# Splitting weight blocks on VectorE alone in the mixers and at the stage ends of a two-block network

## The chip, the core and the metric

The kernel runs on one core of a Trainium2 chip. Five engines work side by side, each on its own queue in order: TensorE (PE; its weight loads are listed as PEld), VectorE (DVE), ScalarE (ACT), GpSimd (POOL) and SyncE (SP, which here only issues loads). Data lie in SBUF, matmul results in PSUM. The metric is the device time of one execution in microseconds, median of several runs.

## The reference

A sequence of 256 rows of width 1024, all in float32, goes through two blocks. The first block has two layers; each is a SwiGLU feed-forward (FFN), a mixer, and a second FFN, each followed by a residual and a layer norm:

```
x = layer_norm(ALPHA * x + 0.5 * swiglu(x, w1, w2))
proj = x @ w_in                       # b_gate, c_gate, v, x_r, y_r, g_logits
y_a = (b_gate * conv3(c_gate * v)) @ w_out_conv
xc  = conv4(x_r) + rc_b;  gates = sigmoid(xc @ rg_w + rg_b)     # per head
y_b = (rg_lru(xc, gates) * gelu(y_r)) @ w_out_rnn
mix = (sigmoid(g_a) * y_a + sigmoid(g_b) * y_b) @ w_o
x = layer_norm(ALPHA * x + mix)
x = layer_norm(ALPHA * x + 0.5 * swiglu(x, w1', w2'))
```

The second block is one layer: modulation, RMS norm, a recurrence and an attention with selected keys, a projection with a residual, and a mixture of 16 experts behind a router in two levels.

## The kernel before

**Weights.** All weights are packed on the host into blocks of 128x1024 floats in the order of their use, two to a load of 1 MB. `Weights.load` (line 161) issues the loads on SP's queue into five raw buffers. A weight is used as a sum of two parts: `Weights.pump` (line 184) takes the next block `h` of the order, has ScalarE cast it to the matmul's type (line 197, the high part) and has VectorE or GpSimd subtract that from the raw block (line 202, the low part). This pair is called a split here. Six split buffers exist (`NSPLIT`); when TensorE is done with a block, `done` (line 272) releases its buffer and pumps the next, so that a split is made some five blocks ahead of its use. A raw buffer is given back when both of its blocks are split. Who subtracts is chosen by three lines of `pump`:

```
pool = self.gp and h % self.gp == 0
if 0 < self.lo <= h < self.lo + len(POOL):
    pool = POOL[h - self.lo] == "1"
```

`gp` is 0 at first: VectorE takes all. `mixer` sets it to `M_GP` = 2 (line 630), so that every second block goes to GpSimd. `tail`, the end of a stage, sets it to 1 (line 467, all to GpSimd) after the first half of the rows, and back to 0 (line 479) where it has begun the next stage. In the last `tail`, in front of the router, it stays 1 until line 1666. `lo` and the 38 digits of `POOL` (line 39) rule the first part of the second block instead.

**Matmuls.** An activation is held as high and low part too, transposed (`xT`: 2 parts x 8 column blocks x 256 rows). `ws` (line 320) multiplies a weight block by it in 24 matmuls of 256 columns: lines 323 to 325 use high x high, high x low, and low x high. `ts` (line 372) and `tz` (line 337) do it the other way round, with 512 columns.

**Mixer** (line 605 on). Two groups of four channel blocks. For two blocks at a time: y_r and x_r are projected; VectorE makes the convolution of four taps (lines 657 and 659), split for the gates by functions put into `soon`, which `done` runs one by one. Then c_gate and v; ScalarE copies one (line 728), VectorE multiplies (line 731), which frees the PSUM tile, and convolves (lines 733, 735). Behind the second of each pair the gate matmuls follow (`gates`, lines 674 to 676), which need PSUM tiles freed by line 731. The recurrence `lru` (lines 684 to 714, with the product by the gelu at line 711) is a generator, advanced by `done` in small steps. The second part of the mixer projects the merge logits, multiplies by the two output matrices (`merge`), and sums into the accumulators with w_o.

**End of a stage** (`tail`, line 435). The last five weight blocks are swept first for rows 0 to 127, then for rows 128 to 255. Between the two, `vec_fn(0)` puts the layer norm of the first half (`ln_vec`, lines 410 to 427) into VectorE's queue: lines 417 and 418 on each half of the columns, a square root on ScalarE, then lines 426 and 427 on each half. The second sweep then pumps new splits as it frees buffers. After it, TensorE transposes the first half (`to_xT`, line 393), ScalarE casts it (line 396) and VectorE makes the low part (line 388). That last step stands in the queue behind the first instructions of the second half's layer norm. `begin` starts the next stage's first four blocks for the first half (line 340), and the second half is transposed. Six stages end this way: FFN, mixer, FFN, twice. At the last of them an RMS norm with its weights follows the layer norm (`rms_in`, lines 505 to 509), and the splits stand in VectorE's or GpSimd's queue ahead of its multiplications (`rest`).

**Router** (`route`, line 1436). In front of the experts, `W.pump(NPRE)` (3 splits) stands ahead of `best_group` (lines 1415 to 1419 and 1426), whose result TensorE ranks (line 1428), and `W.pump(NPRE2)` (2 splits) at the end.

Of the kernel before, what the change touches and what calls it, by code (L numbers as in the profile page):

```python
# [57 lines left out]
ADA = 16  # L58
GATES = (1, 1)
NLAST = 2  # L60
M_WORK, M_GP = 1.2, 2
L_EXP, L_SQ, L_ROOT, L_MUL, L_SCAN = 99, 0.6, 1.0, 2, 0.5
NSPARE = 2
NPRE0, NPRE, NPRE2 = 0, 3, 2
# [166 lines left out]
def kernel(ctx, tc, x, blocks, vecs, lnrows, consts, rows, bias_w, wr, out):  # L231
# [7 lines left out]
    W = Weights(tc, blocks, order, raw_pool, split_pool)  # L239
# [32 lines left out]
    def done(n=1, pump=None, work=None):  # L272
        W.release(n)
        W.pump(n if pump is None else pump)
        if soon:
            soon.popleft()()
        step(M_WORK if work is None else work)
# [35 lines left out]
    def preload(func):  # L313
        nc.scalar.activation(tiny, eps[:, 0:1], func)
# [30 lines left out]
    def begin(keys, xT, mid=None):  # L345
        ps = [mm_tile(), mm_tile()]
        halves = []
        for q in range(4):
            halves.append(W.take(*keys[q]))
            tz(ps[0], 0, halves[q], q, xT)  # L350
            if mid and q == 1:
                mid()
                for k in range(2):
                    tz(ps[1], 1, halves[k], k, xT)
            elif mid and q > 1:
                tz(ps[1], 1, halves[q], q, xT)
        begun.append((ps, halves, xT, mid))
# [77 lines left out]
    def tail(keys, acts, acc, vec_fn, tr_fn, xn=None, plan=None):  # L435
        halves = [W.take(*k) for k in keys]
        last = len(halves) - 1

        def sweep(T, i, n):
            a = acts[i][:, :, T * 128:T * 128 + 128]  # L440
            for hx, hw in ((0, 0), (0, 1), (1, 0)):
                nc.tensor.matmul(acc[T][n], a[:, hx], halves[i][:, hw, n * 512:n * 512 + 512], start=False,
                                 stop=(i == last and hx == 1))

        def spent(T, i):
            if T:
                done(1, pump=int(len(W.split) < (4 if plan else NPRE0)), work=0)

        def half_pass(T, mid=None, rest=None):
            for i in range(last - NLAST + 1):  # L450
                for n in range(2):
                    sweep(T, i, n)
                spent(T, i)
            if rest:
                rest()
            for n in range(2):
                for i in range(last - NLAST + 1, last + 1):
                    sweep(T, i, n)
                    if n:
                        spent(T, i)  # L460
                if mid and n == 0:
                    mid()

        preload(AF.Sqrt)
        half_pass(0)
        rest = vec_fn(0, None)
        W.gp = 1
        if plan:
            half_pass(1, None, rest)
            after = tr_fn(0, mm_tile)  # L470
        else:
            half_pass(1, lambda: tr_fn(0, mm_tile))
            after = None
        rest = vec_fn(1, after)
        if rest:
            rest()
        if plan:
            begin(plan, xn)
            W.gp = 0
            tr_fn(1, acc_tile)()  # L480
        else:
            tr_fn(1, mm_tile)
# [33 lines left out]
    def ffn(l, j, xT, last):  # L516
# [82 lines left out]
        else:  # L599
            vf, tf = (lambda T, mid: ln_vec(T, acc, g, mid)), (lambda T, new: to_xT(xn, xres[:, T], T, new))  # L600
        plan = [("zt", Z_AQ, q) if last else ("em", l, q) if j == 0 else ("e1", l + 1, 0, q) for q in range(4)]
        tail([("w2", l, j, k) for k in ks], [hs[k] for k in ks], acc, vf, tf, xn, plan)
        return xn

    def mixer(l, xT):
# [164 lines left out]
        for i in range(8):  # L770
# [14 lines left out]
            if i >= 2 and i - 2 < 8 - NSTAG:  # L785
# [5 lines left out]
        xn = new_xT()  # L791
        ks = range(8 - NSTAG, 8)
        tail([("wo", l, k) for k in ks], [ms[k] for k in ks], acc, lambda T, mid: ln_vec(T, acc, g, mid),
             lambda T, new: to_xT(xn, xres[:, T], T, new), xn, [("e1", l, 1, q) for q in range(4)])
        return xn
# [683 lines left out]

    ksl = range(nk, 8)  # L1480
    tail([("wout", k) for k in ksl], [mixT[:, :, k] for k in ksl], acc, mix_vec, route)
    turn_[1] = False

# [186 lines left out]
    with tc.If(flag > 0):  # L1670
# [4 lines left out]
        W = W2  # L1675
# [132 lines left out]
```

## Time and profile before

| | |
|---|---|
| median of 3 runs | 1840.64 us (1839.89 to 1840.68) |
| the profiled execution, its own time | 1835.68 us |
| its span, first to last instruction | 1833.9 us |
| TensorE (PE) busy | 1738.9 us, 95% |
| VectorE (DVE) busy | 1304.2 us, 71% |
| ScalarE (ACT) busy | 975.0 us, 53% |
| GpSimd (POOL) busy | 376.9 us, 21% |
| splits on VectorE / GpSimd | 489 + 54 / 122 |
| mean granted TensorE clock | 0.982 |

The profile's times are us from the first instruction. A row of the timeline has the start, the length, the engine, the line of the kernel, the operation, what it writes and reads, the shapes, and in square brackets the engine's idle time before it with what ended it. Busy time of an engine that isn't the bottleneck costs nothing as long as no one waits for it.

### The profile page before, as it was taken

The numbers are of one execution on the slowest core, as the hardware profiler recorded it, in microseconds if no ns is written. First come the engines' busy times: TensorE is split into PE (matmuls) and PEld (weight loads), VectorE is DVE, ScalarE is ACT, GpSimd is POOL, SyncE is SP. The second block draws the span as 40 slices with busy tenths as digits, with TensorE's granted clock in tenths as the row PEclk, the third lists the DMA queues.
The fourth block names the chain that finished last, engine by engine and source line by source line (L and its number), as shares of the span: only waits on it lengthen the run. The fifth ranks groups of instructions, "written<-read, shape, count | busy, mean of one in ns | idle before, by whom it ended". The sixth has DMA issues, their size and how long they took to land. (4 is left out here: it accounts for less than half of the span.)

```text
span 1833.9 us, 27864 instructions
## 1 busy us (share of the span) xinstructions
PE 1738.9 (95%) x11369; PEld 1578.1 (86%) x11369; DVE 1304.2 (71%) x1631; ACT 975.0 (53%) x1340; POOL 376.9 (21%) x195
## 2 busy tenths in 40 slices
PE   8789999999999999999999999999799888999998
PEld 7779899999799989998999997999698666878776
DVE  6276778865856685667788557555778767998997
ACT  5154365644544444444646535444374557777775
POOL 0000144353300020001443543000256541000000
PEclk9989999999999999999999999999899999999999
DMA  7677654555556665675545554655342347989883
GB/s 296 168 266 252 228 173 152 204 190 193 205 183 256 243 236 194 248 257 207 184 161 184 207 185 171 223 184 186 118 172 92 144 169 256 357 323 337 332 318 141
DMA packets 57256, 394.26 MB, mean 215 GB/s; under 512 B 6912, under 2 KB 7216, under 8 KB 10912
## 3 DMA queue, kind: packets, MB, share of 16 engines
q1 hardware_dynamic: 52416, 375.94, 56.1%
q0 software_dynamic: 4128, 15.72, 3.0%
q8 instruction: 91, 1.49, 0.3%
q10 hardware_dynamic: 576, 0.74, 0.1%
q14 instruction: 45, 0.37, 0.1%
HBM read 389.20 MB, written 3.17 MB: 214 GB/s over the span
## 5 line engine op out<-in xcount | busy, mean ns | idle before, releaser
L202 DVE TENSOR_TENSOR split<-raw,split 128x1024 fp32r<-128x1024 f32 x489 | 645.2, 1332 | 298.9 <-ACT split L197 293.8
L197 ACT CAST split<-raw 128x1024 fp32r<-128x1024 f32 x611 | 628.2, 1048 | 248.1 <-PE mm L325 65.1
L202 POOL TENSOR_TENSOR split<-raw,split 128x1024 fp32r<-128x1024 f32 x122 | 317.6, 2613 | 992.3 <-ACT split L197 981.5
L323 PE MATMUL mmo<-xT,split 128*128 128x256 f32 x1248 | 354.1, 284 | 0.0
L324 PE MATMUL mmo<-xT,split 128*128 128x256 f32 x1248 | 353.6, 283 | 0.0
L325 PE MATMUL mmo<-xT,split 128*128 128x256 f32 x1248 | 353.4, 283 | 0.0
L325 PE MATMUL mm<-xT,split 128*128 128x256 f32 x968 | 274.1, 283 | 2.4 <-POOL split L202 2.4
L323 PE MATMUL mm<-xT,split 128*128 128x256 f32 x968 | 274.0, 283 | 0.0
L324 PE MATMUL mm<-xT,split 128*128 128x256 f32 x968 | 273.9, 283 | 0.0
L324 PEld LDWEIGHTS mmo<-xT,split 128*128 128x128 f32 x1248 | 239.6, 192 | 1.7
L323 PEld LDWEIGHTS mmo<-xT,split 128*128 128x128 f32 x1248 | 239.6, 192 | 1.7
L325 PEld LDWEIGHTS mmo<-xT,split 128*128 128x128 f32 x1248 | 239.5, 192 | 0.0
L376 PE MATMUL acc<-split,ht 128*128 128x512 f32 x816 | 199.9, 394 | 16.0 <-ACT split L197 15.8
L376 PEld LDWEIGHTS acc<-split,ht 128*128 128x128 f32 x816 | 149.8, 190 | 46.1 <-ACT split L197 16.0
L1536 PE MATMUL hp<-split,xg 128*128 128x512 f32 x768 | 187.7, 398 | 0.8 <-DVE split L202 0.8
L325 PEld LDWEIGHTS mm<-xT,split 128*128 128x128 f32 x968 | 185.4, 192 | 2.8 <-POOL split L202 2.8
L323 PEld LDWEIGHTS mm<-xT,split 128*128 128x128 f32 x968 | 185.4, 192 | 1.3
L324 PEld LDWEIGHTS mm<-xT,split 128*128 128x128 f32 x968 | 185.4, 192 | 1.3
L1536 PEld LDWEIGHTS hp<-split,xg 128*128 128x128 f32 x768 | 142.9, 188 | 34.8 <-DVE split L202 1.1
L1594 PE MATMUL y<-split,ht 128*128 128x512 f32 x360 | 87.2, 397 | 0.0
L1594 PEld LDWEIGHTS y<-split,ht 128*128 128x128 f32 x360 | 67.1, 188 | 15.8
L553 DVE SCALAR_TENSOR_TENSOR junk<-raw,cb 128x1024 f32<-128x1024 f32 x48 | 58.5, 1219 | 23.2 <-ACT cb L551 23.2
(454 smaller groups left out, 2276.6 us busy)
## 6 DMA issues: line engine op xcount, KB each, us to landing
raw<-in_w_dram SPq DMA_DIRECT2D x328, 1024.0 KB, 4.9
spare<-in_w_dram SPq DMA_DIRECT2D x27, 1024.0 KB, 4.9
lng<-in_ln_dram POOLq DMA_DIRECT2D x6, 1024.0 KB, 4.9
raw<-in_w_dram SPq DMA_DIRECT2D x4, 512.0 KB, 7.7
scr<-ext_s POOLq DMA_DIRECT2D x1, 2048.0 KB, 47.7
cb<-in_row_dram POOLq DMA_DIRECT2D x3, 512.0 KB, 5.6
norm<-mrow POOLq DMA_DIRECT2D x2, 512.0 KB, 4.6
braw<-scr POOLq DMA_DIRECT2D x2, 512.0 KB, 4.8
```

What stands on the lines that cost most here:

```text
L197: self.nc.scalar.copy(t[:, 0], r)
L202: eng.tensor_sub(t[:, 1], r, t[:, 0].bitcast(F32))
L323: nc.tensor.matmul(ps, w[:, 0, k], xT[:, 0, k], start=(k == 0), stop=False)
L324: nc.tensor.matmul(ps, w[:, 0, k], xT[:, 1, k], start=False, stop=False)
L325: nc.tensor.matmul(ps, w[:, 1, k], xT[:, 0, k], start=False, stop=(k == 7))
L376: nc.tensor.matmul(acc[T][n], a[:, hx], half[:, hw, n * 512:n * 512 + 512], start=(first and hx == 0 and hw == 0), stop=(last and hx == 1))
L553: nc.vector.scalar_tensor_tensor(junk, w, 1.0, cb, op0=ALU.mult, op1=ALU.mult, accum_out=modc[:, c:c + 1])
L1536: nc.tensor.matmul(ps, xgs[g][:, hx, k], wv[:, hw, kk], start=(k == 0 and hx == 0 and hw == 0), stop=(k == 7 and hx == 1))
L1594: nc.tensor.matmul(ys[g][n][:, 0:w], ht[:, hx, q], half[:, hw, o:o + w], start=(j == 0 and q == 0 and hx == 0 and hw == 0), stop=(j == 3 a ...
```

## The change

Two lines. `M_GP` becomes 0, so that the mixers give no split to GpSimd, and `tail` no longer sets `gp` to 1. With that, `gp` is 0 everywhere; the string `POOL` still rules its 38 blocks of the second block.

```diff
@@ -58,7 +58,7 @@
 ADA = 16
 GATES = (1, 1)
 NLAST = 2
-M_WORK, M_GP = 1.2, 2
+M_WORK, M_GP = 1.2, 0
 L_EXP, L_SQ, L_ROOT, L_MUL, L_SCAN = 99, 0.6, 1.0, 2, 0.5
 NSPARE = 2
 NPRE0, NPRE, NPRE2 = 0, 3, 2
@@ -464,7 +464,6 @@
         preload(AF.Sqrt)
         half_pass(0)
         rest = vec_fn(0, None)
-        W.gp = 1
         if plan:
             half_pass(1, None, rest)
             after = tr_fn(0, mm_tile)
```

## Rows read from the trace of the kernel before

**Rows 1.** Busy time by engine in two stretches; order PE, PEld, DVE, ACT, POOL, clock, DMA share, GB/s
```profile
240.00:460.00 220.00, 214.30 (x1740) 211.67 (x1739) 157.19 (x183) 121.03 (x178) 96.39 (x39) 1.00 0.52 186
...
971.50:975.00 3.50, 3.50 (x19) 3.50 (x18) 2.92 (x3) 1.53 (x4) 1.80 (x1) 0.51 0.82 300
```

**Rows 2.** Waits of TensorE over the program: us in total, times, longest
```profile
PE mm L393 <- DVE xres L427: 8.5, 4, 2.2
PE mm L393 <- DVE xn L509: 7.3, 1, 7.3
PE rank L1428 <- DVE goh L1419: 6.4, 1, 6.4
...
PE mm L674 <- DVE pc L731: 5.9, 2, 3.0
...
PE mm L325 <- POOL split L202: 4.5, 4, 1.3
```

**Rows 3.** Timeline of the first mixer, VectorE at 262 and 316 to 329 us, GpSimd
```profile
262.60 0.35 DVE L733 TENSOR_SCALAR cv<-pc,vec 128x256 f32<-128x256 f32 x1
...
316.34 2.60 DVE L202 TENSOR_TENSOR split<-raw,split 128x1024 fp32r<-128x1024 f32 x1 [1.05 <-ACT split L197]
...
319.08 2.28 DVE L657 TENSOR_SCALAR xc<-xp,vec 128x256 f32<-128x256 f32 x1
...
326.55 2.39 POOL L202 TENSOR_TENSOR split<-raw,split 128x1024 fp32r<-128x1024 f32 x1 [5.34 <-ACT split L197]
...
326.99 2.09 DVE L733 TENSOR_SCALAR cv<-pc,vec 128x256 f32<-128x256 f32 x1
```

**Rows 4.** Groups of VectorE, 240 to 460 us: count, busy us, mean ns, idle before
```profile
L202 DVE TENSOR_TENSOR split<-raw,split 128x1024 fp32r<-128x1024 f32 x37 | 66.9, 1809 | 46.6 <-ACT split L197 43.6 <-PE mm L325 2.8
L733 DVE TENSOR_SCALAR cv<-pc,vec 128x256 f32<-128x256 f32 x8 | 16.3, 2043 | 0.3
```

**Rows 5.** Groups of VectorE in the experts' stage, 1523 to 1834 us
```profile
L202 DVE TENSOR_TENSOR split<-raw,split 128x1024 fp32r<-128x1024 f32 x133 | 160.4, 1223 | 14.5 <-ACT split L197 12.8
```

**Rows 6.** Busy time of the splits (line 202) in two stretches: DVE, POOL, clock, DMA
```profile
214.00:482.00 268.00, 74.06 (x40) 122.68 (x47) 1.00 0.49 175
661.00:669.50 8.50, 0.00 (x0) 8.40 (x3) 0.90 0.37 125
```

**Rows 7.** Timeline of VectorE, 1127 to 1131 us: four splits in a row
```profile
1126.80 4.63 DVE L202 TENSOR_TENSOR split<-raw,split 128x1024 fp32r<-128x1024 f32 x4 [0.51 <-ACT split L197]
```

**Rows 8.** Timeline of a stage end, 660 to 668 us, VectorE and TensorE
```profile
660.04 0.75 DVE L426 SCALAR_TENSOR_TENSOR lns<-lns,lnmv,lng 128x512 f32<-128x512 f32 x1
...
661.50 2.90 DVE L426 SCALAR_TENSOR_TENSOR lns<-lns,lnmv,lng 128x512 f32<-128x512 f32 x1
...
664.43 2.73 DVE L427 SCALAR_TENSOR_TENSOR xres<-lns,lnmv,lng 128x512 f32<-128x512 f32 x1
...
667.21 0.66 PE L393 MATMUL mmo<-ident,xres 128*128 128x128 f32 x4 [2.08 <-DVE xres L427]
```

**Rows 9.** Timeline of GpSimd, 462 to 486 us, the end of the first mixer
```profile
468.75 10.82 POOL L202 TENSOR_TENSOR split<-raw,split 128x1024 fp32r<-128x1024 f32 x4 [8.15 <-ACT split L197]
```

**Rows 10.** Timeline of VectorE, 1296 to 1332 us, the last stage end of the first block
```profile
1310.56 3.43 DVE L505 TENSOR_TENSOR xn<-xres,norm 128x512 f32<-128x512 f32 x2
...
1323.63 1.29 DVE L505 TENSOR_TENSOR xn<-xres,norm 128x512 f32<-128x512 f32 x2
```

**Rows 11.** Timeline of VectorE, 1495 to 1532 us, the router
```profile
1509.11 1.28 DVE L1416 TENSOR_TENSOR rt<-rlg,rt 128x8 f32<-128x8 f32 x1
1510.42 2.26 DVE L1417 TENSOR_TENSOR rt<-rt,w 128x8 f32<-128x8 f32 x1
...
1512.92 2.06 DVE L1419 TENSOR_TENSOR goh<-w,rt 128x8 f32<-128x8 f32 x1
...
1529.39 0.17 DVE L1417 TENSOR_TENSOR rt<-rt,w 128x8 f32<-128x8 f32 x1
```

## The prediction

> **What bounds the kernel now.** I began with the page's busy times (the table ahead): TensorE is far above the others, so time can only be won where it stands still. Next I cut out the middle of the first mixer: in 220 us TensorE is busy 214.3, VectorE 157.2, GpSimd 96.4 [rows 1]. No helper is full there, and only 5.7 us of standing still can be won in that window. Third, the waits of TensorE over the whole program [rows 2]. Five of them lie where the edited lines act: transposes that wait for the normalised rows of a stage (8.5 us in 4 waits), the same at the last stage of the first block (7.3 us once), the router's ranking (6.4 us once), the gate matmuls of the mixers that wait for VectorE's convolution (5.9 us in 2), and matmuls that wait for a split made on GpSimd (4.5 us in 4). That last one is the only wait that names GpSimd; the others name VectorE.
>
> So the question is why VectorE is late there. Rows of one form, with and without GpSimd beside them, answer it. A 128x256 tensor_scalar at line 733 took 0.35 us at 262.60 us and 2.09 us at 326.99; in the second case a GpSimd split had started at 326.55 and lasted 2.39 us, to 328.94, and the VectorE row ends 0.14 us after that [rows 3]. The same form has a mean of 2043 ns over its eight rows in the window above, and VectorE's own split has 1809 ns [rows 4] against 1223 ns in the experts' stage, where GpSimd splits nothing [rows 5]. VectorE's long rows are thus mostly waits for a GpSimd split to end.
>
> **What the change moves.** Every first-block mixer has 47 GpSimd splits with the stage ends at its two sides [rows 6]; there are two mixers. Two further stage ends have 3 each [rows 6] (the second, at 1304 us, is alike), and the router has 5 (NPRE and NPRE2). That is 94 + 6 + 5 = 105 of the 122. The 17 that the POOL string places in the second block stay. ScalarE's casts, the loads and TensorE's work stay as they are; GpSimd's own DMAs find a free queue; a raw block is given back sooner, which costs nothing as the loads fill 0.52 of the DMA engines here [rows 1]. What is new is that each split stands in VectorE's queue, in program order: 1.22 us alone, 4.63 us for four in a row, so 1.14 us for each further one and 3.49 us for three [rows 5, 7].
>
> **Ends of the first block's FFN stages, three of this kind.** In `tail` VectorE normalises the upper half of the rows while TensorE runs the last sweeps. At 660.04 us an instruction of the chain takes 0.75 us; then GpSimd starts its three splits and the next two take 2.90 and 2.73 [rows 8]. These waits, 2.15 + 1.98 = 4.13 us, go. TensorE's wait of 2.08 us for that result at 667.21 [rows 8] goes too, but this isn't the gain: the three splits now stand on VectorE between the upper half's chain and the lower half's first instruction, and the low part of the transposed rows, which TensorE's first matmuls need, comes after that. This is late next. The chain changes by 3.49 - 4.13 = -0.64 us; three ends: **-1.9 us**.
>
> **Ends of the mixers, two.** Here four splits are pumped [rows 9], so 4.63 - 4.13 = +0.5 us each: **+1.0 us**. This part alone is slower.
>
> **The last stage end.** The same chain, and behind it two multiplications for the RMS norm, which take 3.43 us for the pair with GpSimd running and 1.29 without [rows 10]. They come behind the three splits, so 3.49 - 4.13 - 2.14 = **-2.8 us**; the 7.3 us wait shrinks to about 4.5.
>
> **The router.** `route` pumps three splits ahead of `best_group`. Three tiny instructions of the chain to the group's choice take 1.28, 2.26 and 2.06 us, against 0.17 for the same form later [rows 11]: 5.09 us of waits go, 3.49 us of splits come in front: **-1.6 us**. The last two splits come behind what TensorE waits for; the expert stage's start covers them.
>
> **Inside the mixers.** The waits for GpSimd splits (4.5 us) fall if the split is earlier than now: 1.22 us in place of some 2.4, and its cast earlier too, as ScalarE stands in line behind VectorE's results. The gate wait (5.9 us in 2) hangs on VectorE's chain ahead of it. In the first mixer's stretch from 316 to 329 us the waits are 2.60 - 1.22, 2.28 - 0.35 and 2.09 - 0.35, together 5.0 us [rows 3] (line 657 is priced by line 733's row, both tensor_scalar of one shape), and three splits come in, 3.4 us. Net 1.6 us earlier there, and the stretch ahead carries over more, as its long rows are of the same forms. Bounds: nothing, or all 10.4 us. A loss is not excluded (below). I take all of it, since each of the six waits follows a stretch in which VectorE runs back to back with GpSimd beside it: **-10.4 us**.
>
> **Sum.** -1.9 + 1.0 - 2.8 - 1.6 - 10.4 = -15.7 us. The profiled execution took 1835.68 us, 1.8 more than its span; -15.7 makes it 1820.0. The median of the runs is 1840.64, 5.0 above the profiled one, so **1824.9, say 1825 us**. One thing is left out: behind the second mixer's gate wait the granted clock stood at 0.51, the lower of its two levels (1.2 GHz), for 3.5 us [rows 1], though behind the first mixer's it did not fall. If the fall goes with the wait, 1.7 us more are won.
>
> **Rivals.**
> *The mixers' waits stay* and only take another name: a split is now in line behind VectorE instructions that themselves wait for TensorE or ScalarE, where GpSimd's queue was free. Then 10.4 us are not won: 1840.6 - 5.3 = 1835.3 us. For it: VectorE's split idles 43.6 us for ScalarE's casts in this window [rows 4]. Against it: half of the splits live in that queue today, and a split is made five blocks ahead of its use.
>
> *VectorE becomes the bound inside the mixers* (slower). Place: the three stretches of each mixer that now end in a wait of TensorE. Price: three moved splits of 1.14 us in each, nothing returned, 6 x 3.4 = 20 us; with the -5.3 of the stage ends and the router, 1855 us. It decides where the waits returned are less than 1.14 us for each split moved in. For it: over the 220 us the two forms of that window [rows 4] return 37 x 0.59 + 8 x 1.69 = 35 us, and 38 splits (the 39 GpSimd instructions [rows 1] but for one DMA issue) cost 46 us at 1.22; VectorE goes from 157 to at least 157 + 46 - 35 = 168, or 203 of 220 if nothing came back. Against it: other forms wait too, and in the stretch that counts 5.0 us return for three splits, 1.7 each. The Trainium skill (Perfetto Trace Analysis, Optimizing Scalar/DVE Operations) speaks for this rival: work may be handed from a saturated VectorE to GpSimd; it adds that between these two it might not help, as they share a read port. By its first half the sum would be the 1855 us; by its second half, the 1825. The rows here side with the second half: a VectorE row that ends as the GpSimd split ends.
>
> *More than forecast*: the low clock goes (1.7 us) and some of the transposes' waits too (8.5 us), where the low part of the rows isn't late: 1825 - 10 = 1815 us.
>
> *No change*: the loads, not the splits, set the pace, and what is won is given back: 1840.6. Against it: none of these five waits names a DMA [rows 2]. That the change doesn't do what it says is excluded: both places that set `gp` above 0 go.
>
> **Chances.** Forecast (about 1818 to 1831) 0.60, mixers' waits stay 0.20, more than forecast 0.07, no change 0.05, slower 0.08. Range: 1814 takes in the further gain, 1837 the case that the mixers give nothing; what is left out is the no change, the slower case and an edge. A measurement of this kernel tells some 0.2%, 3.7 us, from no change; the first three cases are faster by more than that: 0.87, the same 0.05, slower 0.08.
>
> **What would show it.** Right: GpSimd with 17 splits; VectorE's split at about 1.22 us in the mixers and line 733 near 0.35; the two STT of a stage end at 0.75 each with three or four splits behind them; the transposes' wait at a stage end replaced by one for the low part of the rows, of some 2 us; the last end's wait near 4.5 and the router's near 4.8; no wait of TensorE in the mixers over 1 us. Wrong: waits of the mixers' matmuls on VectorE's split in place of GpSimd's, longer stage ends than now, or VectorE rows that stay long without a GpSimd split beside them.

## The result, and the profile after

The changed kernel took **1819.31 us** in the median of 4 runs (1817.44 to 1821.13), the kernel before 1840.66 beside it: a ratio of **0.9873** (95% interval 0.9854 to 0.9892), 21 us or 1.3% faster. Measured twice more, beside other runs of the kernel before, it stood at 0.9877 and 0.9866. The forecast of 1825 us was 6 us too high, and its range of 1814 to 1837 us held. The two profiled executions lie closer than the medians: 1835.68 us before and 1821.13 after, 14.6 us. The one of before lies 5 us under its median and the one of after nearly 2 above.

The head of the page after, where the second line shows each engine's busy time and share:

```profile
span 1819.3 us, 27785 instructions
...
PE 1744.1 (96%) x11369; PEld 1583.1 (87%) x11369; DVE 1282.9 (71%) x1736; ACT 977.1 (54%) x1340; POOL 102.2 (6%) x90
```

VectorE has 105 instructions more than before, which are the moved splits, and is busy for less time: 1282.9 us against 1304.2. The middle of the first mixer shows why. Its windows (columns as in [rows 1]), with two stretches at the mixers' ends:

```profile
240.00:460.00 220.00, 220.00 (x1777) 217.35 (x1777) 155.17 (x225) 125.45 (x183) 0.00 (x0) 1.00 0.50 183
472.80:476.30 3.50, 3.50 (x11) 2.68 (x10) 3.03 (x7) 0.29 (x1) 0.00 (x0) 0.51 0.51 211
1104.10:1107.50 3.40, 3.40 (x10) 2.69 (x9) 2.93 (x7) 0.30 (x1) 0.00 (x0) 0.53 0.43 183
```

Two groups of VectorE in the first of these windows:

```profile
L202 DVE TENSOR_TENSOR split<-raw,split 128x1024 fp32r<-128x1024 f32 x76 | 90.8, 1222 | 42.1 <-ACT split L197 42.0
L732 DVE TENSOR_SCALAR cv<-pc,vec 128x256 f32<-128x256 f32 x8 | 2.8, 354 | 0.3
```

TensorE no longer stands still there: 220.0 of 220 us, against 214.3 [rows 1]. VectorE's splits went from 37 to 76 and cost 23.9 us more [rows 4], but its total went from 157.2 to 155.2 us, so all its other work became 25.9 us shorter. Line 732 (733 before) is down from 2043 ns to 354 [rows 4].

The waits of TensorE over the whole program after, us in total, times and longest:

```profile
PE mmo L340 <- DVE xT L388: 7.9, 4, 2.5
...
PE mm L393 <- DVE xn L508: 4.4, 1, 4.4
PE rank L1427 <- DVE goh L1418: 3.8, 1, 3.8
```

The waits of the mixers' matmuls (L674 on the convolution, L325 on GpSimd's split) and of the transposes on `xres` [rows 2] are gone from the list. In place of the last stands one for the low part of the transposed rows, `xT`. This is the timeline of the first mixer's end after:

```profile
465.48 4.62 DVE L202 TENSOR_TENSOR split<-raw,split 128x1024 fp32r<-128x1024 f32 x4
...
470.02 0.68 DVE L417 SCALAR_TENSOR_TENSOR lns<-xres,acc 128x512 f32<-128x512 f32 x1
...
471.34 0.67 DVE L388 TENSOR_TENSOR xT<-mmo,xT 128x512 fp32r<-128x512 f32 x1
...
472.07 6.43 PE L340 MATMUL mmo<-split,xT 128*128 128x512 f32 x20 [2.55 <-DVE xT L388]
```

Four splits in a row, then the lower half's first pair of instructions, and only then the subtract that TensorE waits for. Behind the wait the granted clock stands at 0.51 (the second window above), the lower of its two levels, and twenty matmuls take 6.43 us; the same group took 4.82 us before:

```profile
477.15 4.82 PE L340 MATMUL mmo<-split,xT 128*128 128x512 f32 x20 [0.47 <-DVE xT L388]
```

**Where the time went.** The start of one and the same TensorE instruction in both traces gives the shift of each stage. Below, negative is faster than the profile of before; `after`, c1 and c2 are three profiles of the changed kernel, e1 and e2 its two halves (below).

| stage | forecast | after | c1 | c2 | e1 | e2 |
|---|---|---|---|---|---|---|
| start, first 100 us | 0 | +2.7 | +0.1 | +0.3 | +0.1 | +1.4 |
| first FFN end | -0.6 | -0.7 | -0.4 | -0.6 | +0.1 | -0.4 |
| first mixer | -5.2 | -7.2 | -7.2 | -7.2 | -7.1 | +1.2 |
| its end | +0.5 | +1.7 | +1.7 | +1.7 | -0.1 | +1.5 |
| second FFN end | -0.6 | -1.7 | -1.7 | -1.7 | +0.3 | -1.7 |
| third FFN end | -0.6 | -0.9 | -0.9 | -0.9 | 0.0 | -0.9 |
| second mixer | -5.2 | -8.0 | -8.0 | -8.0 | -8.0 | -0.9 |
| its end | +0.5 | +1.7 | +1.7 | +1.7 | +1.0 | +1.6 |
| start of the last FFN | 0 | -0.4 | -0.4 | -0.4 | -0.4 | -0.4 |
| last FFN and its end | -2.8 | -2.9 | -3.0 | -2.9 | 0.0 | -2.9 |
| second block | 0 | +3.1 | +3.1 | +1.5 | +0.4 | +0.3 |
| router | -1.6 | -2.3 | -1.4 | -2.2 | 0.0 | -1.5 |
| experts | 0 | +0.3 | -0.1 | -0.2 | -0.3 | +0.5 |
| sum | -15.7 | -14.6 | -16.6 | -18.9 | -14.0 | -2.2 |

Down to the last stage end the numbers of the changed kernel repeat to 0.3 us; the start and the second block do not, and they make most of what differs between runs of one kernel.

### The profile page after: what moved, and what is told of

Read it like the earlier page. It is cut to its first block, busy times and chain, and to the rows that moved or that the text cites. A ratio compares the mean times of both kernels' runs of the same rounds, so it can differ in the third digit from the quotient of the medians.

```text
span 1819.3 us, 27785 instructions
## 1 busy us (share of the span) xinstructions
PE 1744.1 (96%) x11369; PEld 1583.1 (87%) x11369; DVE 1282.9 (71%) x1736; ACT 977.1 (54%) x1340; POOL 102.2 (6%) x90
## 5 line engine op out<-in xcount | busy, mean ns | idle before, releaser
L202 DVE TENSOR_TENSOR split<-raw,split 128x1024 fp32r<-128x1024 f32 x594 | 716.8, 1225 | 285.6 <-ACT split L197 283.3
L325 PE MATMUL mmo<-xT,split 128*128 128x256 f32 x1248 | 353.1, 283 | 0.0
L325 PE MATMUL mm<-xT,split 128*128 128x256 f32 x968 | 273.9, 283 | 0.0
L325 PEld LDWEIGHTS mmo<-xT,split 128*128 128x128 f32 x1248 | 239.4, 192 | 0.0
L325 PEld LDWEIGHTS mm<-xT,split 128*128 128x128 f32 x968 | 185.7, 192 | 0.0
L552 DVE SCALAR_TENSOR_TENSOR junk<-raw,cb 128x1024 f32<-128x1024 f32 x48 | 58.5, 1220 | 25.4 <-ACT cb L550 25.4
L202 DVE TENSOR_TENSOR split<-spare,split 128x1024 fp32r<-128x1024 f32 x54 | 65.6, 1223 | 7.8 <-ACT split L197 7.2
```

The source lines that it names most:

```text
L202: eng.tensor_sub(t[:, 1], r, t[:, 0].bitcast(F32))
L325: nc.tensor.matmul(ps, w[:, 1, k], xT[:, 0, k], start=False, stop=(k == 7))
L552: nc.vector.scalar_tensor_tensor(junk, w, 1.0, cb, op0=ALU.mult, op1=ALU.mult, accum_out=modc[:, c:c + 1])
```

## The experiments

**c1: the changed kernel again**, beside the two halves of the change.

> The changed kernel once more, on the chip of the next three. Each theory: 1817 to 1822 us if before gives 1838 to 1842 there; its difference from before is what the two part changes are to add up to.

Measured: 1816.32 us, ratio 0.9877 (0.9861 to 0.9894). The first measurement holds.

**e1: the mixers alone.**

```diff
-M_WORK, M_GP = 1.2, 2
+M_WORK, M_GP = 1.2, 0
```

> GpSimd gives up its splits in the mixers' middle (M_GP = 0) but keeps those of the stage ends and the router. By my theory (VectorE's waits for GpSimd splits) TensorE's six waits in the mixers go, and the two ends of mixers keep their form: -12 to -15 us against before, of which 10.4 are the waits that the trace named. By the rival that the stage ends carry the gain: under -5 us.

Measured: 1824.29 us, ratio 0.9928 (0.9911 to 0.9945), 13.2 us faster, within the 12 to 15 expected. Its waits of TensorE:

```profile
PE mm L393 <- DVE xres L427: 8.5, 4, 2.2
...
PE mm L393 <- DVE xn L509: 7.3, 1, 7.3
PE rank L1428 <- DVE goh L1419: 6.8, 1, 6.8
```

The stage ends' waits stay as in [rows 2], those of the mixers are gone, and the table gives both mixers the same -7 and -8 us as in the whole change. The mixers' gain does not hang on the ends.

**e2: the stage ends and the router alone.**

```diff
         rest = vec_fn(0, None)
-        W.gp = 1
+        W.gp = 0
```

> The stage ends and the router without GpSimd, the mixers' middles with every second split on it, as before. My sum for these parts: -1.9 + 1.0 - 2.8 - 1.6 = -5.3 us; with what the changed kernel's trace showed at the router -6. The rival that the ends carry the gain: -12 or more. Both parts together should give the whole change within 3 us.

Measured: 1833.93 us, ratio 0.9972 (0.9959 to 0.9985), 5.1 us faster. Its waits show the reverse picture:

```profile
PE mmo L340 <- DVE xT L388: 7.9, 4, 2.6
...
PE mm L674 <- DVE pc L731: 5.9, 2, 3.0
PE mm L325 <- POOL split L202: 5.0, 4, 1.3
```

The forecast had -5.3 us for this part. The halves sum to 18.3 us and the whole gave 22.3 (c1), 4.0 apart where at most 3 were expected; the intervals allow that. The mixers, which e2 leaves as they were, moved by +1.2 and -0.9 us in the table; why was not tried.

**e3: GpSimd kept busy beside VectorE.** If VectorE's rows were long because GpSimd worked at the same time, work of GpSimd that nobody needs must bring the loss back.

```diff
             eng.tensor_sub(t[:, 1], r, t[:, 0].bitcast(F32))
+            if self.was and h % self.was == 0:
+                self.extra(t)
...
+            nc.gpsimd.tensor_copy(spare[:, 1, 0:1], t[:, 1, 0:1].bitcast(F32))
+            nc.gpsimd.tensor_sub(spare[:, 0], spare[:, 0], spare[:, 1])
```

> The changed kernel, with GpSimd put back beside VectorE where the mixers' first part runs: for every second block GpSimd subtracts two SBUF tiles of 128x1024 that no one waits for, started when VectorE has made the split. All splits stay on VectorE. My theory: VectorE's rows get long again (tensor_scalar of the convolution over 1 us in the mean, splits over 1.5 us), VectorE, busy 81% there without waits, takes on some 20 waits of over 1 us per mixer and TensorE waits: +8 to +30 us over the changed kernel. The rival (late blocks: a split takes 2.4 us on GpSimd and 1.2 on VectorE, and nothing else counts): within 3 us of the changed kernel, as no split is on GpSimd.

Measured: 1876.0 us, ratio 1.0205 (1.0187 to 1.0222), 60 us over the changed kernel (c1) and twice the upper end expected; the two mixers alone are 28.7 and 29.7 us longer than in `after`. The groups of VectorE and GpSimd in this run, 231 to 390 us:

```profile
L202 DVE TENSOR_TENSOR split<-raw,split 128x1024 fp32r<-128x1024 f32 x45 | 69.3, 1562 | 5.8 <-ACT split L197 5.8
L320 DVE TENSOR_TENSOR xch<-xc,xch 128x256 fp32r<-128x256 f32 x8 | 12.2, 1519 | 0.0
L665 DVE TENSOR_SCALAR xc<-xp,vec 128x256 f32<-128x256 f32 x8 | 11.8, 1475 | 0.4
L667 DVE SCALAR_TENSOR_TENSOR xc<-xp,vec,xc 128x256 f32<-128x256 f32 x24 | 11.6, 485 | 0.9
L717 DVE TENSOR_TENSOR_SCAN xc<-aa,gi 128x256 f32<-128x256 f32 x8 | 9.4, 1215 | 0.0
...
L636 POOL TENSOR_TENSOR spare<-spare 128x1024 f32<-128x1024 f32 x22 | 62.3, 2830 | 1.8
```

No split is late through GpSimd here, ScalarE's waits in this stretch name TensorE and VectorE only, and yet VectorE is full: its rows stretch while GpSimd runs. L667, which reads two SBUF tiles, keeps its 485 ns, but that says nothing of GpSimd: by the timeline none of its 24 rows ran beside a subtract, and at four of the eight places the tensor_scalar ahead of them had waited one out. The first of these:

```profile
238.25 2.41 POOL L636 TENSOR_TENSOR spare<-spare 128x1024 f32<-128x1024 f32 x1
...
238.26 2.55 DVE L665 TENSOR_SCALAR xc<-xp,vec 128x256 f32<-128x256 f32 x1
240.84 1.53 DVE L667 SCALAR_TENSOR_TENSOR xc<-xp,vec,xc 128x256 f32<-128x256 f32 x3
```

The rival that lateness alone counts falls. The small copy that starts each subtract is not the cause either, since e4 has it too.

**e4: GpSimd writes only.** The subtract becomes `nc.gpsimd.memset(spare, 0.0)` over both halves.

> The changed kernel, and beside the mixers GpSimd again works on a spare tile that nobody waits for, 22 times a mixer as in the run with the subtracts, but it only writes there (a memset of 128x2048, 1.81 us each) in place of a 128x1024 subtract (2.83 us each); nothing is left out. Theory: VectorE's rows with two inputs from SBUF wait for a GpSimd instruction that itself reads, so that it is the reading subtract that costs; with the memset the 128x1024 split of VectorE stays near 1.22 us, tensor_scalar L732 near 0.35, and the time within 4 us of the changed kernel (1815 to 1821). Rival: any work of GpSimd stops them; then 22 x 1.81 us lie beside VectorE in each mixer instead of 22 x 2.83, its splits go to 1.4 us or more and the time rises by 25 to 45 us. Rival: VectorE loses nothing and what cost 60 us was the small copy that starts GpSimd; then it is 60 here as well.

Measured: 1819.24 us, ratio 0.9879 (0.9861 to 0.9896), the time of the changed kernel. The groups, 231 to 365 us:

```profile
L202 DVE TENSOR_TENSOR split<-raw,split 128x1024 fp32r<-128x1024 f32 x46 | 55.2, 1220 | 12.0 <-ACT split L197 12.0
...
L665 DVE TENSOR_SCALAR xc<-xp,vec 128x256 f32<-128x256 f32 x8 | 6.6, 827 | 3.2 <-ACT xp L660 2.9
L717 DVE TENSOR_TENSOR_SCAN xc<-aa,gi 128x256 f32<-128x256 f32 x8 | 5.1, 675 | 0.0
...
L636 POOL MEMSET spare<- 128x2048 f32 x22 | 39.9, 1812 | 1.3
```

With 39.9 us of GpSimd's writing beside it the split stays at 1220 ns. The tensor_scalar rows did wait, against the expectation: 827 ns, where `after` has 410 (L656), and 632 ns at L741, where it has 354 (L732). These are sixteen rows in a mixer, and each mixer was 0.9 us longer than in `after`.

**e10: GpSimd reads one tile** and copies it, between e3 and e4: `nc.gpsimd.tensor_copy(spare[:, 0], spare[:, 1])`.

> As the run with GpSimd's subtracts, but GpSimd copies one half of the spare tile to the other: it reads one tile and not two, 128x1024 each; nothing is left out. Theory: what stops VectorE's two-input rows is that GpSimd reads by the same way, and one reader is enough: the 128x1024 split goes above 1.4 us and the time up by 15 to 50 us. Rival: only a GpSimd instruction that reads two tiles stops them; then the split stays at 1.22 us and the time within 4 us of the changed kernel, as with the memset.

Measured: 1828.22 us, ratio 0.9933 (0.9909 to 0.9957), 12 us over the changed kernel (c2) by the ratios; below the 15 expected for one reader, and far from none. The groups, 231 to 370 us:

```profile
L202 DVE TENSOR_TENSOR split<-raw,split 128x1024 fp32r<-128x1024 f32 x46 | 60.8, 1340 | 11.7 <-ACT split L197 11.7
...
L717 DVE TENSOR_TENSOR_SCAN xc<-aa,gi 128x256 f32<-128x256 f32 x8 | 6.7, 882 | 0.0
...
L636 POOL COPY spare<-spare 128x1024 f32<-128x1024 f32 x22 | 30.9, 1405 | 1.3
```

The split loses 46 x 0.118 = 5.4 us to 30.9 us of copies, and 45 x 0.340 = 15.3 us to 62.3 us of subtracts in e3. One reader is enough; the copy is half as long as the subtract.

**e5: the rival that was slower.** VectorE gets 22 more subtracts of 128x1024 in each mixer, and GpSimd nothing: `nc.vector.tensor_sub(spare[:, 0], spare[:, 0], spare[:, 1])` in the place of e3's pair.

> The changed kernel, with VectorE doing one more 128x1024 subtract on a spare tile behind every second split of a mixer's first part (22 a mixer, 1.22 us each by the split's own row, 26.9 us); GpSimd does nothing there, nothing is left out. Theory: what the run with GpSimd's subtracts lost is VectorE's time, which is full there; VectorE has 101.7 us of work in 126 us of a mixer now, 128.5 with these, and at the 93% that it reached in that run a mixer takes 138 us, 12 more: +24 us in all, 10 to 32. Rival: VectorE's fullness does not count and only its lateness through GpSimd does; then the 24 us of idle time hold it and the time is within 4 us of the changed kernel.

Measured: 1835.70 us, ratio 0.9968 (0.9955 to 0.9981), 18 us over the changed kernel's mean ratio of 0.9872. The window 231 to 357 us of `after`:

```profile
231.00:357.00 126.00, 125.76 (x1028) 124.51 (x1027) 101.67 (x166) 84.87 (x128) 0.38 (x1) 1.00 0.51 186
```

The same window of e5:

```profile
231.00:357.00 126.00, 123.21 (x1005) 121.31 (x1004) 117.21 (x177) 81.81 (x125) 0.00 (x0) 1.00 0.47 170
```

VectorE is at 81% after the change and has room. With 26.8 us more it is at 93%, and TensorE stands still: each mixer takes 10 us more than in `after`. So the change had room for its splits only since the other rows came back.

**e6: the xT subtracts first.** At a stage end `mid()`, which issues the two L388 subtracts, moves ahead of the lower half's first L417 and L418.

```diff
+            if n == 0 and mid:
+                mid()
             nc.vector.scalar_tensor_tensor(s[:, sl], xres[:, T, sl], ALPHA, acc[T][n], op0=ALU.mult, op1=ALU.add)
             nc.vector.bn_stats(st[:, n], s[:, sl])
-            if n == 0 and mid:
-                mid()
```

> The changed kernel, and at the ends of the stages the two L388 subtracts of the first half's xT stand ahead of the second half's first L417 and L418 on VectorE, not behind them: 0.68 + 0.69 us sooner for the next product, the same instructions. Theory: the waits for xT at three FFN ends (1.41 us) and two mixer ends (2.55 us) each lose 1.35 us, and the half clock behind the two 2.55 us waits goes with them (3.4 us at half speed, some 1.6 us each): -10 us, and -6.8 if the clock falls all the same. Rival: the second half's normalisation comes later by as much and the time is the same, within 2 us. Nothing is left out.

Measured: 1815.10 us, ratio 0.9857 (0.9840 to 0.9874), 3 us under the changed kernel's mean ratio, not the 7 to 10 expected, and inside the uncertainty. TensorE at the first stage end in `after`:

```profile
225.04 4.82 PE L340 MATMUL mmo<-split,xT 128*128 128x512 f32 x20 [1.41 <-DVE xT L388]
229.69 0.60 PE L393 MATMUL acc<-ident,xres 128*128 128x128 f32 x4
230.61 0.66 PE L393 MATMUL acc<-ident,xres 128*128 128x128 f32 x4 [0.32 <-DVE xres L427]
```

And in e6:

```profile
219.51 6.12 PE L340 MATMUL mmo<-split,xT 128*128 128x512 f32 x24 [0.24 <-ACT xT L396]
226.25 0.66 PE L393 MATMUL acc<-ident,xres 128*128 128x128 f32 x4 [0.61 <-DVE xres L427]
227.70 0.66 PE L393 MATMUL acc<-ident,xres 128*128 128x128 f32 x4 [0.79 <-DVE xres L427]
```

The wait of 1.41 us goes and comes back as 0.61 and 0.79 us for the lower half's rows. At the FFN ends the rival was right: VectorE's chain of splits and normalisation sets when the stage ends, in whatever order. At the two mixer ends the clock no longer falls, and they win 1.5 and 1.6 us in the profile, with 0.4 given back behind the second.

**e8: the router's chain first.** Of the three splits ahead of `best_group`, two go behind it.

```diff
-        W.pump(NPRE)
+        W.pump(1)
         best_group()
...
-        W.pump(NPRE2)
+        W.pump(NPRE - 1 + NPRE2)
```

> The changed kernel, and in the router two of the three splits ahead of the best-group chain go behind it. Theory: the chain starts some 2.3 us sooner (two splits of 1.18 us), the matmul on rank waits 1.5 us instead of 3.8, and the time falls by 2 to 2.4 us; the splits come 2.4 us later, when the experts' first product has other splits in hand. Rival: the experts' first products wait for those splits, and the time is within 1 us of the changed kernel. Nothing is left out.

Measured: 1815.08 us, ratio 0.9861 (0.9842 to 0.9879), 2 us under the changed kernel's mean ratio, again inside the uncertainty. The trace has it beyond doubt: the wait on `rank`, 3.8 us after the change, is

```profile
1492.40 0.59 PE L1427 MATMUL rank<-goh,kc 128*128 128x4 f32 x2 [1.60 <-DVE goh L1418]
```

and the router's stage is 3.7 us shorter than before, where the changed kernel's profiles have 1.4 to 2.3.

**c2, e9 and e7: the changed kernel once more, both orders together, and the mixers' ends back on GpSimd.** e7 sets `gp` to 1 in `tail` when a mixer calls it, and to 0 otherwise.

> The changed kernel itself, as the measure for the two orders beside it: 1816 to 1820 us, ratio near 0.9875.

> The changed kernel with both orders that helped alone: the L388 subtracts of the first half ahead of the second half's normalisation, and the router's best-group chain ahead of two splits. They touch different ends, so the gains add: about 3 us and 2.5 us, 5.5 us under the changed kernel in the same call (3 to 7). Rival: they share an end and only the larger shows, 3 us. Nothing is left out.

> The changed kernel, but at the ends of the two mixers all splits go to GpSimd again, as in the kernel before; nothing is left out. Theory: these two ends are the part of the change that costs, 1.7 us each in the profiles (2.5 us waits for xT with half clock behind them), so this kernel is 3.4 us faster than the changed one; no wait of 2.5 us for xT stands at 472 and 1103 us and the clock is full behind them. Rival: the normalisation is late again by the GpSimd splits (4.1 us an end) and the time is the same or up to 2 us longer.

Measured: c2 1816.82 us, 0.9866 (0.9849 to 0.9883); e9 1814.05 us, 0.9857 (0.9841 to 0.9873); e7 1819.07 us, 0.9887 (0.9871 to 0.9904). e9 has the lowest median of the three, 2.8 us under c2, half of the 5.5 expected and near the 3 of its rival, and the intervals overlap: that it beats the changed kernel is likely and not shown. The rival's reason doesn't hold, since the trace has both gains: the mixers' ends are as short as in e6, and the router's stage is 3.5 us shorter than before. e7 was expected 3.4 us under c2 and was 2.3 over it; so its theory isn't borne out by the time, and its intervals overlap too. Its trace is mixed: against `after` the mixers' ends are 1.0 and 1.8 us shorter, 0.4 us is given back behind the second, and at the first the clock fell all the same, as this window shows:

```profile
469.20:472.60 3.40, 3.40 (x10) 2.52 (x9) 3.33 (x6) 0.59 (x1) 3.40 (x2) 0.51 0.75 301
```

## Why the prediction was right, and where its sizes were off

**The mechanism is shown.** The step on which all rested, that VectorE's long rows are waits for a GpSimd split, holds: with GpSimd's splits gone the rows of [rows 4] and [rows 8] are short (354 ns for 2043; both L426 of the stage end of [rows 8] at 0.75 us, as below), and subtracts that nobody needs bring long rows back (e3).

```profile
656.55 0.75 DVE L426 SCALAR_TENSOR_TENSOR lns<-lns,lnmv,lng 128x512 f32<-128x512 f32 x1
...
658.01 0.75 DVE L426 SCALAR_TENSOR_TENSOR lns<-lns,lnmv,lng 128x512 f32<-128x512 f32 x1
```

What stops the splits is narrower than the prediction could see: not any work of GpSimd, but its reading of SBUF (e3, e10, e4). The Trainium skill (SBUF — State Buffer, Who interferes with whom) states just this: a VectorE instruction with two SBUF inputs contends with a GpSimd instruction that reads SBUF, not with one that only writes. The runs agree: 1562 and 1340 ns beside a reading GpSimd, 1220 beside a writing one, 1222 alone. The tensor_scalar rows, with which the prediction argued first, are another kind: they read one tile and columns of factors, and GpSimd's writing stretches them too (827 ns in e4, 1475 in e3, 410 in `after`). One thing stays open: for the four mixer waits that name a GpSimd split (at most 1.3 us each), its own length of some 2.4 us against 1.22 on VectorE would almost be enough, and no run separates that from VectorE's long rows.

**The mixers: right, and undersized.** Forecast -10.4, which was also its upper bound, and measured -15.1 in the trace and -13.2 (-10.1 to -16.4) in e1. Three things were missing in the term, and the first is the price of a wait, which was taken as the idle time shown. These are TensorE's rows around the first mixer's gate wait in the kernel before:

```profile
328.44 0.28 PE L676 MATMUL mmo<-xch,split 128*128 128x256 f32 x1
331.67 0.39 PE L674 MATMUL mm<-xch,split 128*128 128x256 f32 x1 [2.95 <-DVE pc L731]
331.89 0.28 PE L675 MATMUL mm<-xch,split 128*128 128x256 f32 x1
332.01 0.28 PE L676 MATMUL mm<-xch,split 128*128 128x256 f32 x1
```

Undisturbed, these matmuls start every 0.12 us. From 328.44 to 331.89 are two steps, 0.24 us, that took 3.45: the wait cost 3.21, not 2.95. Counted so, the six waits come to 11.9 us. That is 1.5 us more. The low clock behind the second mixer's gate wait, which the forecast left out, is 1.4 us. Four waits of 0.15 to 0.23 us that it did not count cost the last 1.8.

**The stage ends of the FFNs** were forecast at -0.64 each; two came at -0.4 to -0.9. The second has -1.7, since before the clock had fallen behind its wait of 2.08 us [rows 8], as this window of before shows, and after it does not:

```profile
667.50:671.00 3.50, 3.50 (x12) 2.52 (x11) 3.43 (x6) 0.58 (x1) 1.90 (x1) 0.54 0.29 87
```

**The last end** (-2.8) came at -2.9, with the wait of 4.4 us as forecast. **The router** (-1.6) came at -1.4 to -2.3; its wait is 3.8 to 4.6 us in the three profiles, where 4.8 was forecast.

**The mixers' ends: right sign, size off.** +0.5 each was forecast and +1.7 measured. The step that failed is the sum of VectorE's instructions alone. It had the late `xT` right, but not what stands behind a wait of 2.5 us: 3.4 us at half clock, some 1.6 us at each end in all three profiles of the changed kernel. e6, where the wait is 1.24 us, has no fall and these ends at +0.1.

**The rivals.** "The mixers' waits stay" is out: no wait of TensorE of over 0.3 us is left inside a mixer. "VectorE becomes the bound" stands on the right place and the wrong return. It counted 35 us given back in 220 for the two forms shown, but all the other rows gave back 25.9 and the 37 old splits 21.7, together 47.6 us against the 47.7 that 39 new splits cost. That a loss would have come without that return is what e5 speaks for: there 26.8 us that nothing returned cost 10 us a mixer. "More than forecast" asked for waits of the stage ends to go; they did not, and the further gain came from the mixers.

**What was luck.** That the profile of `after` gives -14.6, close to the sum of -15.7, is in part luck: the mixers gave 4.8 us more than forecast and their ends took 2.4 of it back, and the start and the second block, which the change does not touch, took another 5.8. The other two profiles gave -16.6 and -18.9. The medians gave -21 to -24.5; they lie further off mainly because the one profiled execution of before was itself 3 to 6 us under the medians of before. Why it was so short was not tried.

**Open.** The second block, which the change does not touch, is 1.5 to 3.1 us longer in the three profiles of the changed kernel and 0.3 to 5.9 us longer in all the other runs, so the one profile of before may have been short there. The mean granted clock in it is 0.95 before, 0.93 in `after` and 0.97 in c2, which does not order the three. What makes it vary was not tried.

## What to carry to other kernels

Before a helper is given half of a busy engine's work, compare that engine's rows with and without the helper running: here VectorE did all the splits itself in the time that it had lost to waiting. Look at what the helper does, not only at how long it runs: 39.9 us of writes cost a mixer 0.9 us, and 62.3 us of subtracts, which read, cost 29. And when an engine takes work back, follow what is queued behind that work, since the gain at a stage end shrank to the time of the splits placed ahead of the next result.

## What was not expected of the hardware

A memset of GpSimd leaves the splits, with two SBUF inputs, alone but does stretch tensor_scalar (410 to 827 ns in e4). The scan, which also reads two SBUF tiles, went from 675 to 1215 ns beside GpSimd's subtracts. The waiting goes both ways: in these rows of e3 VectorE's product started 0.03 us ahead of GpSimd's subtract and kept its 1.23 us, and the subtract took 3.43 us instead of the 2.41 above:

```profile
309.71 1.23 DVE L719 TENSOR_TENSOR xc<-xc,gely 128x1024 f32<-128x1024 f32 x1
...
309.74 3.43 POOL L636 TENSOR_TENSOR spare<-spare 128x1024 f32<-128x1024 f32 x1
```

And the same wait is not always followed by the low clock: the mixers' ends of e8 are those of the changed kernel, but at the second one the clock stays full behind a wait of 2.55 us, and this end comes at +0.1 and not +1.7. Its TensorE row, and the window behind the wait:

```profile
1101.25 4.88 PE L340 MATMUL mmo<-split,xT 128*128 128x512 f32 x20 [2.55 <-DVE xT L388]
...
1101.30:1104.70 3.40, 3.40 (x15) 2.78 (x16) 2.94 (x7) 0.29 (x1) 0.00 (x0) 1.00 0.69 292
```

So the low clock behind these waits is a risk and no fixed price, which is the likely reason that e6, e7 and e9 could not be told from the changed kernel by their times. That was argued and not shown.
